# Where the first four activation tiles begin in on-chip memory: 96 instead of 128 modulo 256 bytes

## The chip, the core and the metric

The kernel runs on one core of one Trainium2 chip. The metric is the device time of one execution in microseconds, as the median over runs. TensorE does the matrix products, VectorE, ScalarE and GpSimd the elementwise work, and SyncE issues most of the DMAs. A granted clock of 1.00 in the profile is TensorE's upper level, 2.4 GHz; the lower one is 1.2 GHz.

## What is computed

Two transformer blocks run over one sequence of 256 positions of width 2048, everything in float32. The first mixes by pooling and a gated delta rule, attends to a memory of 256 rows, and ends in a gated feed-forward layer of width 5632. The second mixes by two sparse attentions and ends in a feed-forward layer of width 8192. Cut to its large products:

```python
x = x + hybrid_mixer(rms_norm(x, g1), w_in, ...) # h @ w_in, then y @ w_mix_out
x = x + memory_cross_attention(rms_norm(x, g2), mem_h, w_xq, w_xkv, w_xo)
x = x + (silu(causal_dwconv(h @ w_gate, cw, cb)) * (h @ w_up)) @ w_down
x = rms_norm(x, final_norm_g)
...
o = concat([nsa_mixer(...), moba_mixer(...)]) @ w_o    # inputs from h @ w_in_2
x = x + gate_m * rms_norm_2(o, post_norm_mix)
x = x + gate_f * rms_norm_2(square(relu(h @ w_up_2)) @ w_down_2, post_norm_ffn)
```

## The kernel before

**Products.** Every large product is made of three single-pass products in the type float32r: each operand is split into a high part and a low remainder, and high x high, high x low and low x high are summed in PSUM. Weights arrive by DMA in units of 128x1024 float32 (`load_to`, L202), ScalarE writes the high part `wh` (L216), VectorE the low part `wl` (L218).

**Two ways round.** `lin_b` (L316 to L318) has a 128x128 block of the weights as the stationary operand and streams 256 columns of an activation row past it: `wh` against the high part of the activations, `wh` against the low part, `wl` against the high part. `lin_a` (L298 to L300) has 128 columns of the activations as the stationary operand and streams 512 columns of `wh` or `wl` past them (256 in the last two groups of three layers). Each matmul is preceded by its own weight load, which the profile lists as engine PEld. A group is one block of 512 output columns; over a contraction of 2048 it has 192 matmuls in `lin_b` and 96 in `lin_a`.

**Activation tiles.** `act_pair(0)` hands out the tiles A0 to A3 (high part in A0 and A1, low part in A2 and A3), `act_pair(1)` the tiles A4 to A7. Each is 128x8x256 of float32, 8192 bytes in a partition, and a row that `lin_b` streams is 1024 bytes of it. A0 to A3 hold the input of `w_in`, of `w_xq`, of `w_gate` and `w_up`, of `w_in_2` and of `w_up_2`, which all go through `lin_b` except the `z`, `nv` and `mv` parts; they also hold the mixer's output, which is the stationary operand of `w_mix_out`. A4 to A7 hold the lifted memory (streamed by the four groups of keys, `mk`, and stationary for `mv`), the attention outputs and the hidden units of both feed-forward layers, which are stationary in `w_xo`, `w_down`, `w_o_2` and `w_down_2`.

**Places.** The pool gives every name its bytes in the order in which the program first asks for it, rounded up to 32 bytes in a partition, and keeps them. Counted so, the built program puts `mhalf` at byte 54400, `c_first` at 54432, the three columns `c_G1`, `c_G2` and `c_GP` (64 bytes each, asked for early, L572, and used much later) at 54464, 54528 and 54592, then A0 at 54656, which is 128 modulo 256. A1, A2 and A3 follow without a gap, so that all their rows begin at 128 modulo 256. Then come `c_mix_p` and `c_mem_p` (32 bytes each), and A4 at 87488, which is 192 modulo 256; so are A5, A6 and A7. The three buffers of `wh` and the three of `wl` all begin at 192 modulo 256, and a stationary block in them is 512 bytes further each.

**Order.** Instructions are written in the order in which they run on each engine. While a group's matmuls are issued, `pump` slips in pieces of the other work (the evacuation of earlier groups, the adaptive gains, the delta rule).

Of the kernel before, what the change touches and what calls it, by code (L numbers as in the profile page):

```python
# [18 lines left out]
KB = D // P  # L19
# [71 lines left out]
class Prog:  # L91
# [407 lines left out]
    def run(self):  # L499
# [69 lines left out]
        self.mhalf = self.pool.tile([P, 8], F32, name="mhalf")  # L569
        nc.gpsimd.memset(self.mhalf, -0.5)  # L570
        nc.scalar.activation(self.col("first", 8), self.mhalf, AF.Copy)
        for name in ("G1", "G2", "GP"):  # L572
            self.col(name, KB)


        self.split_to(1)
# [9 lines left out]
        def stats():  # L586
            nc.sync.dma_start(cst, i["cst"])
            for c in range(4):
                nc.sync.dma_start(self.X[:, :, c * 512:(c + 1) * 512], xsrc[:, :, c * 512:(c + 1) * 512])
                yield  # L590
            self.load_small(w_in, 5120, 16, "ba", "s9")
            for n in ("dn_a_log", "dn_dt_bias"):
                t = self.named[n] = self.col(n, 8)
                sv = i[n]
                nc.sync.dma_start(t, bass.AP(tensor=sv.tensor, offset=sv.offset, ap=[[0, P], [1, 8]]))
            self.load_const("early")
            for c in range(4):
                for tb in range(2):
                    self.sq_sum(self.X[:, tb, c * 512:(c + 1) * 512], parts[:, tb, c:c + 1])
                yield  # L600
            yield from self.rms_task("mix_r", parts, "rr")
            msrc = i["mem"][0].rearrange("(b p) d -> p b d", p=P)
            for c in range(4):
                mt = self.t("r7", [P, 2, 512])
                nc.gpsimd.dma_start(mt, msrc[:, :, c * 512:(c + 1) * 512])
                for _ in range(3):
                    yield
                for tb in range(2):
                    self.sq_sum(mt[:, tb], mparts[:, tb, c:c + 1])
            self.rcm = self.rms_cols("mem_r", mparts)  # L610
            yield
            self.rrm = yield from self.row_bcast(self.rcm, "rrm", 1)

        st = self.start(stats())
        A4 = self.t("A4", [P, 2, 4, T])
        A5 = self.t("A5", [P, 2, 4, T])
        for name in ("silu_c", "gl16"):
            self.col(name, KB)
        S = [{"k": A4[:, 0], "q": A4[:, 1], "v": A5[:, 0]}, {}]
        self.z = [None, None]  # L620
# [650 lines left out]
    def ffn1(self, xh, xl, ready, rt):  # L1271
# [6 lines left out]
        def ups(s):  # L1278
            hid[s] = self.hidden(["A4", "A6"] if s % 2 else ["A5", "A7"])
            j = 0  # L1280
            for c in self.slabs[s]:
                self.lin_b(self.gate[c], xh, xl, lambda a, c=c: self.chain(self.wait_for(rt), self.gate_evac(a, c)),
                           ready=ready if c == 0 else None)
                self.lin_b(self.up[c], xh, xl, lambda a, c=c, j=j: self.up_evac(a, c, j, hid[s]))
                j += 4
# [141 lines left out]
    def mixer2(self):  # L1427
# [48 lines left out]
        ev = self.lin_a(b2["nv"], xh, xl, lambda a: self.copy2_evac(a, vsw))  # L1476
        o0h, o0l = self.hidden(["A4", "A6"])
        att = []
# [401 lines left out]
    def ffn2(self):  # L1880
# [8 lines left out]
        def ups(s):  # L1889
            hid[s] = self.hidden(["A4", "A6"] if s % 2 else ["A5", "A7"])  # L1890
            for c in range(2 * s, 2 * s + 2):
                self.lin_b(self.up2[c], xh, xl, lambda a, c=c: self.relu_evac(a, c, hid[s]),
                           ready=ready if c == 0 else None)
# [89 lines left out]
```

## Time and profile before

| what | us |
|---|---|
| median of 3 runs | 2738.76 |
| lowest and highest run | 2735.97, 2741.46 |
| the profiled execution | 2730.08 |
| its span, first to last instruction | 2728.3 |
| PE busy within the span | 2678.7 |

The profiled execution is one more run. Its time is its span plus 1.8 us; it lies 8.7 us below the median. In the profile PE counts a matmul from its start to its end, and neighbouring matmuls overlap; how fast a stream of them runs is read from the distance between their starts, called the pitch below.

### The profile page before, as it was taken

How to read it: one execution, taken by the hardware profiler on the slowest of the kernel's cores; microseconds unless marked ns; L12 is line 12 of the kernel's file. 1: busy time of each engine (PE TensorE's matmuls, PEld its weight loads, DVE VectorE, ACT ScalarE, POOL GpSimd, SP SyncE). 2: the span in 40 equal slices, each digit the busy share in tenths (PEclk: the TensorE clock that was granted, in tenths of full speed). 3: DMA queues.
4: the chain of work that ended last, by engine and by line, in shares of the span. 5: the costliest groups of instructions: out<-in, count | busy, mean ns of one | idle time of the engine just before them, and what ended most of it. 6: DMA issues, size and time to landing. Idle time of an engine off the chain costs nothing.

```text
span 2728.3 us, 45974 instructions
## 1 busy us (share of the span) xinstructions
PE 2678.7 (98%) x18466; PEld 2476.8 (91%) x18466; DVE 1852.9 (68%) x2327; ACT 1303.5 (48%) x1924; POOL 256.4 (9%) x234
## 2 busy tenths in 40 slices
PE   8999999999999999999999989999989999999998
PEld 8999998889989999999999789997889988999897
DVE  6665745677688877777877576677675566655555
ACT  6544533454455454444444554444554444444443
POOL 0230211000000021000000001001011000000020
PEclk9999999999999999999999999999989999999999
DMA  8644644688788888888887656544557767766654
GB/s 293 197 131 132 187 123 141 217 295 274 225 269 273 284 262 262 280 271 267 287 265 256 196 157 179 147 147 131 170 178 234 237 218 239 233 191 192 189 186 151
DMA packets 293127, 584.33 MB, mean 214 GB/s; under 512 B 21921, under 2 KB 36385, under 8 KB 292913
## 3 DMA queue, kind: packets, MB, share of 16 engines
q1 hardware_dynamic: 288528, 568.41, 65.4%
q0 software_dynamic: 3664, 11.67, 1.4%
q8 instruction: 145, 2.38, 0.3%
q10 hardware_dynamic: 720, 1.31, 0.1%
q14 instruction: 70, 0.57, 0.1%
HBM read 579.21 MB, written 2.10 MB: 213 GB/s over the span
## 4 chain that ended last, share of the span: by engine, by line
PE 91%; DVE 3%; ACT 2%; issue 2%; DMA 1%; POOL 1%; SPq 0%; DVEq 0%; POOLq 0%; ACTq 0%
PE acc L316 16%; PE acc L318 16%; PE acc L317 16%; PE acc L298 12%; PE acc L299 12%; PE acc L300 12%; DVE wl L218 1%; ACT wh L216 1%; DMA w<-w_in 1%; PE m L996 1%; PE m L1049 1%; PE m L1056 1%; ACT dd L376 1%; PE m L1146 1%; PE m L1115 1%
## 5 line engine op out<-in xcount | busy, mean ns | idle before, releaser
L218 DVE TENSOR_TENSOR wl<-w,wh 128x1024 fp32r<-128x1024 f32 x880 | 1096.2, 1248 | 811.6 <-ACT wh L216 809.6
L216 ACT ACTIVATE wh<-w 128x1024 fp32r<-128x1024 f32 x880 | 928.1, 1058 | 1111.3 <-PE acc L317 603.3
L316 PE MATMUL acc<-A,wh 128*128 128x256 f32 x3968 | 1122.6, 283 | 9.4 <-ACT A L404 7.7
L318 PE MATMUL acc<-A,wl 128*128 128x256 f32 x3968 | 1111.3, 280 | 6.2 <-DVE wl L218 6.2
L317 PE MATMUL acc<-A,wh 128*128 128x256 f32 x3968 | 1111.0, 280 | 0.7 <-DVE A L1423 0.7
L318 PEld LDWEIGHTS acc<-A,wl 128*128 128x128 f32 x3968 | 756.2, 191 | 8.0 <-DVE wl L218 8.0
L316 PEld LDWEIGHTS acc<-A,wh 128*128 128x128 f32 x3968 | 749.7, 189 | 11.4 <-ACT A L404 7.7
L317 PEld LDWEIGHTS acc<-A,wh 128*128 128x128 f32 x3968 | 749.3, 189 | 2.6 <-DVE A L1423 1.2
L298 PE MATMUL acc<-wh,A 128*128 128x512 f32 (+1 forms) x1584 | 616.0, 389 | 0.3 <-DVE r L1262 0.3
L299 PE MATMUL acc<-wl,A 128*128 128x512 f32 (+1 forms) x1584 | 608.0, 384 | 1.1 <-DVE wl L218 0.9
L300 PE MATMUL acc<-wh,A 128*128 128x512 f32 (+1 forms) x1584 | 607.7, 384 | 0.0
L299 PEld LDWEIGHTS acc<-wl,A 128*128 128x128 f32 x1584 | 298.1, 188 | 60.2 <-DVE wl L218 4.2
L300 PEld LDWEIGHTS acc<-wh,A 128*128 128x128 f32 x1584 | 297.7, 188 | 59.3
L298 PEld LDWEIGHTS acc<-wh,A 128*128 128x128 f32 x1584 | 297.9, 188 | 57.2 <-issue 0.9
L1198 DVE SCALAR_TENSOR_TENSOR r<-r,c_silu_c,r 128x1024 f32<-128x1024 f32 x128 | 170.0, 1328 | 0.0
L1874 POOL TENSOR_TENSOR s<-s 128x512 f32<-128x512 f32 x32 | 51.0, 1592 | 582.5 <-ACT s L1873 582.5
L1198 DVE SCALAR_TENSOR_TENSOR s<-s,c_silu_c,s 128x512 f32<-128x512 f32 x128 | 95.8, 748 | 13.7 <-DMA s<-w_ada 12.4
L1253 POOL TENSOR_TENSOR r<-r,rr 128x1024 f32<-128x1024 f32 x11 | 27.8, 2532 | 565.7 <-ACT r L1252 565.7
L1718 ACT ACTIVATE s<-s,c_am 128x128 f32<-128x128 f32 (+1 forms) x48 | 21.5, 448 | 92.0 <-DVE c_am L1716 92.0
L1606 POOL TENSOR_TENSOR r<-r,s 128x512 f32<-128x512 f32 x15 | 25.6, 1704 | 269.6 <-DVE s L1603 269.6
L1249 DVE SCALAR_TENSOR_TENSOR r<-r,prm,r 128x254 f32<-128x254 f32 x88 | 42.4, 481 | 1.6
L376 ACT ACTIVATE dd<-X 128x512 bf16<-128x512 f32 (+1 forms) x42 | 25.5, 608 | 36.1 <-DVE X L1458 16.1
(376 smaller groups left out, 1611.0 us busy)
## 6 DMA issues: line engine op xcount, KB each, us to landing
w<-w_up SPq DMA_DIRECT2D x216, 512.0 KB, 3.8
w<-w_down SPq DMA_DIRECT2D x216, 512.0 KB, 4.0
w<-w_in SPq DMA_DIRECT2D x152, 512.0 KB, 3.7
r<-w_ada SPq DMA_DIRECT2D x128, 512.0 KB, 5.1
w<-w_gate SPq DMA_DIRECT2D x88, 512.0 KB, 4.2
w<-w_xkv SPq DMA_DIRECT2D x64, 512.0 KB, 3.9
s<-w_ada SPq DMA_DIRECT2D x128, 256.0 KB, 5.2
w<-w_mix_out SPq DMA_DIRECT2D x32, 512.0 KB, 3.7
```

The lines of the kernel that those rows point to most:

```text
L216: nc.scalar.activation(hi[:, :m], src[:, :m], AF.Copy)
L218: eng.tensor_tensor(lo[:, :m], src[:, :m], hi[:, :m].bitcast(F32), op=OP.subtract)
L298: mm(ps, h, wh[:, k, :], start=kb == 0, stop=False)
L299: mm(ps, h, wl[:, k, :], start=False, stop=False)
L300: mm(ps, lo, wh[:, k, :], start=False, stop=kb == g.nkb - 1)
L316: mm(ps, wb, h, start=kb == 0 and b % 2 == 0, stop=False, skip_group_check=True)
L317: mm(ps, wb, lo, start=False, stop=False, skip_group_check=True)
L318: mm(ps, wb2, h, start=False, stop=kb == g.nkb - 1, skip_group_check=True)
L376: self.nc.scalar.activation(junk[:, :src.shape[-1]], src, AF.Square, accum_out=out)
L1198: nc.vector.scalar_tensor_tensor(acc, tiles.pop(n), self.silu_c[:, kb:kb + 1], acc, op0=OP.mult, op1=OP.add)
L1249: nc.vector.scalar_tensor_tensor(cv[:, b, s:], st[:, b, :T - s], w[k], cv[:, b, s:], op0=OP.mult, op1=OP.add)
L1874: nc.gpsimd.tensor_tensor(y, y, y, op=OP.mult)
```

## The change

Two of the early requests are exchanged. Of the three columns ahead of A0 the third, `GP` (64 bytes), is replaced by `ffn_p` (32 bytes), a column that is otherwise asked for much later; `GP` is now placed where the program first uses it. So A0 to A3 begin 32 bytes earlier, at 54624 and on, which is 96 modulo 256. After A3 and the two columns that follow it, `xa_p` (32 bytes) is asked for ahead of A4, so that A4 stays at 87488. The remaining small columns shift by 32 or 64 bytes; `mod` is among them, at 96 modulo 256 instead of 128. All other large tiles, `wh`, `wl` and the landing buffers of the weights keep their places. On every engine the instructions, their order and their waits are the same as before.

```diff
@@ -569,8 +569,8 @@
         self.mhalf = self.pool.tile([P, 8], F32, name="mhalf")
         nc.gpsimd.memset(self.mhalf, -0.5)
         nc.scalar.activation(self.col("first", 8), self.mhalf, AF.Copy)
-        for name in ("G1", "G2", "GP"):
-            self.col(name, KB)
+        for name, n in (("G1", 16), ("G2", 16), ("ffn_p", 8)):
+            self.col(name, n)
@@ -612,6 +612,8 @@
         st = self.start(stats())
+        for name, n in (("xa_p", 8),):
+            self.col(name, n)
         A4 = self.t("A4", [P, 2, 4, T])
         A5 = self.t("A5", [P, 2, 4, T])
```

## Rows read from the trace of the kernel before

**Rows 1.** The page, parts 1 and 2: busy time, granted clock.

```profile
PE 2678.7 (98%) x18466; PEld 2476.8 (91%) x18466; DVE 1852.9 (68%) x2327; ACT 1303.5 (48%) x1924; POOL 256.4 (9%) x234
...
PEclk9999999999999999999999999999989999999999
```

**Rows 2.** The page, part 4: the chain that ended last, by engine, line.

```profile
PE 91%; DVE 3%; ACT 2%; issue 2%; DMA 1%; POOL 1%; SPq 0%; DVEq 0%; POOLq 0%; ACTq 0%
PE acc L316 16%; PE acc L318 16%; PE acc L317 16%; PE acc L298 12%; PE acc L299 12%; PE acc L300 12%; DVE wl L218 1%; ACT wh L216 1%; DMA w<-w_in 1%; PE m L996 1%; PE m L1049 1%; PE m L1056 1%; ACT dd L376 1%; PE m L1146 1%; PE m L1115 1%
```

**Rows 3.** The page, part 5: count, busy us, mean ns, idle before.

```profile
L316 PE MATMUL acc<-A,wh 128*128 128x256 f32 x3968 | 1122.6, 283 | 9.4 <-ACT A L404 7.7
L318 PE MATMUL acc<-A,wl 128*128 128x256 f32 x3968 | 1111.3, 280 | 6.2 <-DVE wl L218 6.2
L317 PE MATMUL acc<-A,wh 128*128 128x256 f32 x3968 | 1111.0, 280 | 0.7 <-DVE A L1423 0.7
...
L298 PE MATMUL acc<-wh,A 128*128 128x512 f32 (+1 forms) x1584 | 616.0, 389 | 0.3 <-DVE r L1262 0.3
```

**Rows 4.** Tile A: count, durations in ns, first and last start; three stretches.

```profile
L316 PE MATMUL acc<-A,wh x64: 276/276/367, 31.8 to 55.0; 128*128 128x256 f32 x64
...
L317 PE MATMUL acc<-A,wh x220: 276/276/276, 1394.8 to 1469.3; 128*128 128x256 f32 x110
...
L318 PE MATMUL acc<-A,wl x64: 276/276/276, 2427.8 to 2449.3; 128*128 128x256 f32 x64
```

**Rows 5.** The same view, four other stretches.

```profile
L317 PE MATMUL acc<-A,wh x31: 281/281/281, 84.3 to 94.9; 128*128 128x256 f32 x31
...
L316 PE MATMUL acc<-A,wh x254: 281/281/281, 980.3 to 1069.7; 128*128 128x256 f32 x127
...
L318 PE MATMUL acc<-A,wl x126: 281/281/281, 2137.8 to 2181.9; 128*128 128x256 f32 x126
...
L317 PE MATMUL acc<-A,wh x63: 281/281/281, 2604.7 to 2626.6; 128*128 128x256 f32 x63
```

**Rows 6.** Timeline of PE in the keys' first group: start us, duration us.

```profile
299.83 0.28 PE L317 MATMUL acc<-A,wh 128*128 128x256 f32 x1
...
300.19 0.28 PE L317 MATMUL acc<-A,wh 128*128 128x256 f32 x1
...
300.55 0.28 PE L317 MATMUL acc<-A,wh 128*128 128x256 f32 x1
...
300.91 0.28 PE L317 MATMUL acc<-A,wh 128*128 128x256 f32 x1
```

**Rows 7.** Tile A in the last group, 256 weight columns wide.

```profile
L298 PE MATMUL acc<-wh,A x16: 283/283/283, 2710.7 to 2716.1; 128*128 128x256 f32 x16
```

**Rows 8.** Chain in order of time, a `w_down_2` group: start us, us, what.

```profile
2094.16 0.23 PE acc L298
...
2104.36 0.23 PE acc L298
```

**Rows 9.** The same view, a `w_mix_out` group.

```profile
497.08 0.23 PE acc L298
...
507.38 0.23 PE acc L298
```

**Rows 10.** Lines L258 and L260, a small projection, 65 to 76 us.

```profile
L258 PE MATMUL m<-A,s x12: 276/276/276, 65.8 to 73.7; 128*32 128x256 f32 x12
...
L260 PE MATMUL m<-A,s x12: 276/276/276, 65.9 to 73.8; 128*16 128x256 f32 x12
```

**Rows 11.** Busy time by engine in two stretches of `w_gate` and `w_up`.

```profile
core 0: us, PE busy (x) PEld busy (x) DVE busy (x) ACT busy (x) POOL busy (x), PEclk, DMA share, GB/s
870.00:956.00 86.00, 86.00 (x761) 86.00 (x761) 71.39 (x75) 42.15 (x46) 4.30 (x3) 1.00 0.86 294
980.00:1070.00 90.00, 90.00 (x765) 89.92 (x764) 72.01 (x72) 41.99 (x46) 8.95 (x5) 1.00 0.84 271
```

**Rows 12.** Waits of PE: us in total, times, longest.

```profile
PE acc L316 <- ACT A L404: 7.7, 1, 7.7
...
PE acc L318 <- DVE wl L218: 6.2, 9, 0.8
```

## The prediction

> **What bounds the kernel now.** Read the busy shares and the chain first. PE is busy for 2678.7 of 2728.3 us at the upper clock level [rows 1], the chain is 91% PE, and 48% of it is the three lines of `lin_b`, 36% those of `lin_a` [rows 2]. PE hardly waits: the two largest waits of these lines are 7.7 us, once at the start, and 6.2 us in nine pieces [rows 12]. In the gate and up stages VectorE is busy 71.4 of 86 us and ScalarE 42.2 [rows 11]. `lin_b` has 3968 matmuls in each of its three lines [rows 3], 11,904; 768 of them are the keys', and 11,136 stream A0 to A3. So the time is the number of matmuls times their pitch, and the change can act only on that pitch: there is nothing else in it.
>
> Next, the pitch itself. The 256-column matmuls of `lin_b` with A0 to A3 have two pitches. In some stretches each lasts 276 ns and 220 of one line start within 74.5 us: 74.5 / 219 / 3 = **113.4 ns** [rows 4]. In others it is 281 ns, and (1069.7 - 980.3) / 253 / 3 = **117.8 ns** [rows 5]. Tiles, code and clock are the same; a stretch keeps its pitch over whole groups, and a change mostly falls where the stream was interrupted. Taking the view group by group, 22 of the 58 groups that stream A0 to A3 are at the short pitch (the first and last are in rows 4) and 36 at the long one (first and last in rows 5): 22 x 192 = 4224 and 36 x 192 = 6912 matmuls.
>
> **Why a start address can matter here.** Four places differ in where the two operands begin. I write the distance as stationary start minus streaming start, in bytes.
> - Distance 0, both at 192: the keys stream A4 to A7 against `wh`; three matmuls take 0.36 us, 120.0 ns each [rows 6]. The last group streams 256 columns of `wh` against A4 to A7: (2716.1 - 2710.7) / 15 / 3 = 120.0 ns [rows 7]. With 512 columns it is (2104.36 - 2094.16) / 15 / 3 = 226.7 ns [rows 8]. The 256 further columns cost 106.7 ns, 0.417 ns each, so that a fixed 13.3 ns, or 32 columns, come on top of each matmul.
> - Distance +64 (stationary `wh` at 192, A0 to A3 streaming at 128): 113.3 or 117.8 ns, so the fixed part is 6.7 or 11.1 ns, and 64 bytes (16 columns, 6.7 ns) have saved all of themselves or a third.
> - Distance -64 (stationary A0 to A3 at 128, `wh` streaming at 192): (507.38 - 497.08) / 15 / 3 = 228.9 ns [rows 9], a fixed part of 15.6 ns: a third of 64 bytes on top.
>
> An estimate from these rows: the fixed part falls with the distance, by its full column time in the short mode and a third of it in the long one. A place of its own speaks against it: the small projection loads 32 or 16 stationary columns from 192 and 64 in turn, and streams A0 to A3 at the short 276 ns throughout [rows 10] (its tile `s10` begins at 192, and each step is 128 bytes). That the stationary start counts at all rests on rows 9 against rows 8.
>
> The Trainium skill says otherwise ("TensorE: Matmul & The Clock Gate", Part 2, step-by-step): TensorE reads the streaming operand and the next weights through two independent ports, and loading does not take bandwidth from the running matmul. By that the start of the streaming operand alone would count, which is the first rival below; rows 8 and 9, which share the streaming start and differ by 2.3 ns, do not agree with it.
>
> **The change part by part.**
> 1. *A0 to A3 streaming at 96 in `lin_b`.* The distance becomes +96, 24 columns or 10.0 ns. Short mode: 13.3 - 10.0 = 3.3 ns, pitch 110.0, which is 3.33 ns less for 4224 matmuls: -14.1 us. Long mode: 13.3 - 10.0 / 3 = 10.0 ns, pitch 116.7, 1.11 ns less for 6912: -7.7 us. No row has a start that is not a multiple of 64, so the bounds lie at the nearest rows and past them. Above: the 120.0 ns of distance 0 [rows 6]. Below: 106.7 ns, no fixed part at all, 11,136 matmuls x (116.1 now on the mean - 106.7) = -105 us. I take the value that continues the rows, because 96 is the near neighbour of 128.
> 2. *A0 to A3 stationary at 96 in `lin_a`.* `z0`, `z1`, `w_mix_out`, `nv` and two `mv` groups have 192 + 384 + 288 = 864 matmuls. The distance goes from -64 to -96, another sixth of 6.7 ns: +1.1 ns, +1.0 us. Bounds: -2.3 ns (distance 0) and +6.7 ns, -2 to +6 us.
> 3. *ScalarE and VectorE writing the rows of A0 to A3, and the moved columns.* These are the same instructions; VectorE has some 15 us in 86 to spare [rows 11]. The columns are single small operands. I cost them at nothing; without that cover, VectorE's 71.4 us would have to grow by a fifth before it set the pace.
>
> Sum: -14.1 - 7.7 + 1.0 = **-20.8 us**. On the profiled execution 2730.1 - 20.8 = 2709.3; the median was 8.7 us above that execution, which is what some 2000 matmuls more at the long pitch would cost (2000 x 4.45 = 8.9). Since the share of modes is that of one execution, I put the gain on the median: 2738.8 - 20.8 = **2718**. Its own range, with a share of the short mode (now 4224 of 11,136) from a fifth to a half and 6.67 ns between the modes, is 2709 to 2731.
>
> **The rivals.**
> - *A start off the 64-byte grid costs a whole extra piece* (slower). Against streaming at 128, streaming at 192 adds 6.7 ns to the short pitch, and both are multiples of 64; 96 is halfway into such a piece. If what counts is the streaming start alone and any start that is not a multiple of 128 reads one piece more, A0 to A3 behave like A4 to A7 in rows 6: 120.0 ns. 4224 x 6.67 + 6912 x 2.22 = 28.2 + 15.3 = +43.5 us, 2782. If the unused 96 bytes count in full (24 columns over the 6.7 ns at 128, 16.7 ns, pitch 123.3): 4224 x 10 + 6912 x 5.56 = +80.6, 2819. For it: the exact 120.0 with two streaming operands. Against: rows 9. It decides from a pitch above 116.1, today's mean.
> - *The modes change, the pitches do not.* All groups short: 6912 x 4.45 = -30.8 us, 2708; all short at 110.0 ns: -67.9, 2671. All long at 117.8: 4224 x 4.45 = +18.8, 2757. For it: the same code has both modes, so a small push decides which is entered. Against: nothing says which way.
> - *Nothing happens at 32 bytes*: 2739. The Trainium skill gives on-chip memory lines of 16 bytes ("SBUF — State Buffer", Specifications); 96 and 128 both begin such a line, and by it alone the change would do nothing. The rows with 128 and 192, both such starts too, differ by 6.7 ns. What speaks for this rival in the rows is that the small projection kept one pitch over two stationary starts [rows 10].
>
> **How the numbers follow.** Forecast (both modes a little shorter) 0.32, 2709 to 2731; the short mode takes all 0.18, 2671 to 2708; all long 0.08, 2757; the extra piece at 120.0 ns 0.20, 2782, and at 123.3 ns 0.08, 2819; nothing 0.14, 2739. About 0.2%, 5.5 us, is what a measurement of this kernel can tell from no change. Faster: 0.32 x 0.95 + 0.18 = 0.48; same: 0.14 + the edge of the forecast = 0.16; slower: 0.08 + 0.28 = 0.36. The range 2675 to 2790 leaves out the all-short end (0.05), 123.3 ns (0.08) and some 0.05 of what is not listed.
>
> **What would show it.** In the same view of tile A, calm stretches of `lin_b` with durations below 276 ns and a pitch near 110.0, others near 116.7, and the `w_mix_out` group near 230 ns, show steps 1 and 2 right. A single duration of 283 ns and a pitch of 120.0 in the gate and up stages show the extra piece. 276 and 281 unchanged, with other shares, show that only modes moved. The pitch of `w_down` and `w_down_2` (226.7) and of the keys (120.0) must not change in any case, since A4 to A7 and `wh` stay. The prediction is wrong if the streaming start alone counts, or if VectorE's or ScalarE's writes to A0 to A3 slow enough to make PE wait.

## The result, and the profile after

The change makes the kernel slower: the median goes from 2737.38 (four runs, the three of above and one more) to **2755.18 us**, a ratio of **1.0064**, with a 95% interval of 1.0047 to 1.0082. I had forecast 2718. The four runs after lie between 2754.99 and 2757.21; the runs of before in the same comparison between 2735.97 and 2741.46. The profiled execution after took 2755.07 us, its span is 2753.2. Against the span of before, 2728.3, that is +24.9 us; the medians differ by 17.8, because the profiled execution of before lay 7.3 us below its median and that of after lies at its own.

The page of the kernel after, part 1 and the clock of part 2, as in [rows 1]:

```profile
PE 2705.9 (98%) x18466; PEld 2500.1 (91%) x18466; DVE 1852.7 (67%) x2327; ACT 1303.7 (47%) x1924; POOL 255.4 (9%) x234
...
PEclk9999999999999999999999999999999999999999
```

PE is busy 27.2 us longer in as many instructions, at the same clock; VectorE, ScalarE and GpSimd are busy as long as before, to 1 us. PE does not wait longer: its waits (us in total, times, longest), the two that [rows 12] shows, are

```profile
PE acc L316 <- ACT A L404: 7.7, 1, 7.7
...
PE acc L318 <- DVE wl L218: 5.5, 9, 0.8
```

Part 5 of the page (count, busy us and mean ns, idle before), as in [rows 3]:

```profile
L316 PE MATMUL acc<-A,wh 128*128 128x256 f32 x3968 | 1127.5, 284 | 9.2 <-ACT A L404 7.7
L318 PE MATMUL acc<-A,wl 128*128 128x256 f32 x3968 | 1116.4, 281 | 5.5 <-DVE wl L218 5.5
L317 PE MATMUL acc<-A,wh 128*128 128x256 f32 x3968 | 1115.9, 281 | 0.7 <-DVE A L1425 0.7
...
L298 PE MATMUL acc<-wh,A 128*128 128x512 f32 (+1 forms) x1584 | 617.1, 390 | 0.3 <-DVE r L1264 0.3
```

So the time went where the prediction said that it had to go, into the pitch of `lin_b`, but with the other sign. Tile A in four calm stretches of the kernel after, that is, with nothing slipped in between the matmuls (count, durations shortest/median/longest, first and last start): a `w_up` group, a `w_up_2` group, a `w_mix_out` group, a `w_down` group:

```profile
L317 PE MATMUL acc<-A,wh x65: 277/281/283, 1015.8 to 1038.6; 128*128 128x256 f32 x65
...
L317 PE MATMUL acc<-A,wh x65: 277/280/282, 2070.4 to 2092.9; 128*128 128x256 f32 x65
...
L299 PE MATMUL acc<-wl,A x16: 392/392/392, 502.2 to 512.7; 128*128 128x512 f32 x16
...
L298 PE MATMUL acc<-wh,A x16: 389/389/389, 1107.2 to 1117.4; 128*128 128x512 f32 x16
```

The single durations of 276 and 281 ns [rows 4, 5] are gone; one stretch now mixes 277 to 283. The pitch is (1038.6 - 1015.8) / 64 / 3 = **118.7 ns** in the first and (2092.9 - 2070.4) / 64 / 3 = **117.2 ns** in the second; in before both groups were at the long pitch, 117.8. All 32 calm groups that stream A0 to A3 sit near one of these two values (26 at 118.7 and 6 at 117.3 by their means), and they are not the long and the short ones of before: of ten groups that were short, seven are now at 118.7 and three at 117.3. `w_mix_out` went from 228.9 [rows 9] to 10.5 / 15 / 3 = 233.3 ns. `w_down` keeps 10.2 / 15 / 3 = 226.7 ns [rows 8], and the keys keep 120.0: in the timeline (start, duration)

```profile
303.39 0.28 PE L317 MATMUL acc<-A,wh 128*128 128x256 f32 x1
...
303.75 0.28 PE L317 MATMUL acc<-A,wh 128*128 128x256 f32 x1
...
304.11 0.28 PE L317 MATMUL acc<-A,wh 128*128 128x256 f32 x1
```

Summed over groups, each from its first to its last start, after minus before:

| groups | us |
|---|---|
| the 22 groups of `lin_b` that were short before (4224 matmuls) | +16.9 |
| the 36 that were long (6912) | +5.8 |
| `lin_a` with A0 to A3 stationary (864) | +1.0 |
| `lin_a` with A4 to A7, and the keys | +1.1 |
| the rest, between the groups | +0.1 |
| span | +24.9 |

### The profile page after: what moved, and what is told of

Read it like the earlier page. It is cut to its first block, busy times and chain, and to the rows that moved or that the text cites. A ratio compares the mean times of both kernels' runs of the same rounds, so it can differ in the third digit from the quotient of the medians.

```text
span 2753.2 us, 45974 instructions
## 1 busy us (share of the span) xinstructions
PE 2705.9 (98%) x18466; PEld 2500.1 (91%) x18466; DVE 1852.7 (67%) x2327; ACT 1303.7 (47%) x1924; POOL 255.4 (9%) x234
## 4 chain that ended last, share of the span: by engine, by line
PE 89%; DVE 4%; ACT 2%; issue 2%; DMA 1%; POOL 1%; SPq 1%; DVEq 0%; POOLq 0%; ACTq 0%
PE acc L316 16%; PE acc L318 16%; PE acc L317 16%; PE acc L298 12%; PE acc L299 12%; PE acc L300 11%; DVE wl L218 2%; ACT wh L216 1%; PE m L998 1%; PE m L1051 1%; DMA s<-w_ada 1%; PE m L1058 1%; DMA w<-w_in 1%; ACT dd L376 1%; PE m L1117 1%
## 5 line engine op out<-in xcount | busy, mean ns | idle before, releaser
L317 PE MATMUL acc<-A,wh 128*128 128x256 f32 x3968 | 1115.9, 281 | 0.7 <-DVE A L1425 0.7
L317 PEld LDWEIGHTS acc<-A,wh 128*128 128x128 f32 x3968 | 750.8, 189 | 2.6 <-DVE A L1425 1.2
```

What stands on the lines that cost most here:

```text
L317: mm(ps, wb, lo, start=False, stop=False, skip_group_check=True)
```

## The experiments

The kernels differ from before in the list of columns that are asked for ahead of A0 and ahead of A4, and in the size of a tile called `spare`, allocated ahead of the weight buffers: with 48 floats of it `wh` and `wl` begin at 192 modulo 256, each 8 floats less move them down by 32 bytes. "Distance" is the prediction's: stationary start minus streaming start, counted modulo 256. The theory that I carried from the result was that this distance decides; the rival, that the streaming start alone does. Each kernel up to the distance of +80 ran once. Beside it stands before on the same chip: one run of 2735.98 us for the first three kernels and for the start at 64, one of 2734.63 for the other four, and for +80 the median of 13 runs, 2735.82. Runs of before alone lie between 2730 and 2742 us, so that a single time says something from about 10 us on; the pitches are read from the traces.

**The moved columns alone.** Four columns ahead of A0, so that it stays at 128:

```diff
-        for name in ("G1", "G2", "GP"):
-            self.col(name, KB)
+        for name, n in (("G1", 16), ("G2", 16), ("ffn_p", 8), ("xa_p", 8)):
+            self.col(name, n)
```

> The small columns move as in the change (GP late, ffn_p and xa_p ahead of A0, mod at 96), but A0 to A3 stay at 128 modulo 256. If the tiles' start is the cause, lin_b has the two pitches of before, 113.3 and 117.8 ns, the w_mix_out groups 229 ns, and the time is that of before (2736 to 2741 us). If a moved column is the cause, the pitches of the change, 117.3 and 118.7 ns, or its time, 2755 us, come back.

Measured: 2733.8 us against 2735.98, and both pitches of before. The same view, a `w_up` group and a stretch at the short duration:

```profile
L317 PE MATMUL acc<-A,wh x64: 280/281/282, 1006.6 to 1028.8; 128*128 128x256 f32 x64
...
L317 PE MATMUL acc<-A,wh x220: 275/276/281, 1394.8 to 1469.7; 128*128 128x256 f32 x110
```

(1028.8 - 1006.6) / 63 / 3 = 117.5 ns, the long pitch; the second stretch has an interruption in it, and its calm groups are at 113.3. The moved columns cost nothing that shows; the start of A0 to A3 is the cause.

**The change, and the weights 32 bytes lower too.** A0 to A3 at 96 as in the change, `wh` and `wl` at 160: distance +64 again.

```diff
-        for name in ("G1", "G2", "GP"):
+        for name, n in (("G1", 16), ("G2", 16), ("ffn_p", 8)):
...
+        for name, n in (("xa_p", 8),):
...
-        self.pool.tile([P, 48], F32, name="spare")
+        self.pool.tile([P, 40], F32, name="spare")
```

> The change, with wh and wl (and the landing buffers) 32 bytes earlier too, at 160: A0 to A3 still begin at 96, but the distance from streaming to stationary start is +64 again. If the distance decides: lin_b back at 113.3 and 117.8 ns, w_mix_out back at 229 ns; the keys (distance -32) above 120 ns, near 121 to 123; w_down and w_down_2 (distance +32) below 226.7 ns, near 223 to 226; about 2715 to 2735 us. If the start of the streaming operand alone decides: lin_b stays at 117.3 and 118.7 ns, keys at 120.0, and all lin_a groups move alike to one new pitch.

**The other way.** A0 to A3 stay at 128, `wh` and `wl` go to 224: distance +96 without the change.

```diff
-        self.pool.tile([P, 48], F32, name="spare")
+        self.pool.tile([P, 56], F32, name="spare")
```

> The kernel before, with wh and wl 32 bytes later, at 224: A0 to A3 stay at 128, the distance becomes +96 as in the change. If the distance decides: lin_b at 117.3 and 118.7 ns and w_mix_out at 233.4 ns as after the change; the keys (distance +32) below 120 ns, w_down and w_down_2 (distance -32) above 226.7, near 228; 2755 to 2765 us. If the streaming start alone decides: lin_b at 113.3 and 117.8 ns.

Measured: 2736.9 us for the first, 2777.35 for the second. First kernel, a `w_up`, a `w_up_2` and a `w_down` group; then the second kernel, a `w_up` and a `w_down` group:

```profile
L317 PE MATMUL acc<-A,wh x65: 276/276/276, 1006.0 to 1027.8; 128*128 128x256 f32 x65
...
L317 PE MATMUL acc<-A,wh x65: 281/281/281, 2165.5 to 2188.1; 128*128 128x256 f32 x65
...
L299 PE MATMUL acc<-wl,A x16: 395/396/396, 1095.0 to 1105.5; 128*128 128x512 f32 x16
```

```profile
L317 PE MATMUL acc<-A,wh x65: 276/281/283, 1018.7 to 1041.5; 128*128 128x256 f32 x65
...
L299 PE MATMUL acc<-wl,A x16: 393/394/397, 1110.8 to 1121.3; 128*128 128x512 f32 x16
```

With A0 to A3 at 96 and the distance back at +64, the two pitches of before return: 21.8 / 64 / 3 = 113.5 and 22.6 / 64 / 3 = 117.7 ns. With A0 to A3 untouched and the distance at +96, the pitch is 22.8 / 64 / 3 = 118.7, that of the change. This settles it: the distance decides, not the place of either operand alone. (The landing buffers of the weights move with `wh` and `wl`, but PE's waits are those of before.) Both kernels pay in `w_down`, where A4 to A7 stayed and the weights moved: 10.5 / 15 / 3 = 233.3 ns in place of 226.7, some 19 us over all groups of `lin_a` with A4 to A7. That is why the first, whose `lin_b` with A0 to A3 is 11.5 us quicker than in the profile of before, does not gain. Here the expectations missed: 223 to 226 ns at distance +32 and 228 at -32 were too low, the keys at -32 ran near 116.7 and not above 120, and the second kernel came out 12 us above its range.

**All large operands 32 bytes lower**, so that every distance stays (the change without `xa_p` ahead of A4, and `spare` with 40 floats, so that A4 to A7, `wh` and `wl` are at 160).

> The change with A4 to A7 and wh and wl 32 bytes earlier as well: every large operand begins off the 64-byte grid (96 and 160), and all distances are those of before. If the distance alone decides: 113.3 and 117.8 ns, keys 120.0, w_mix_out 229, w_down 226.7, 2725 to 2741 us by the share of the two pitches. If a start off the 64-byte grid costs by itself: 117.3 and 118.7 ns or more in lin_b and 233.3 ns in lin_a, 2755 to 2775 us.

Measured: 2731.75 us against 2734.63, a `w_up` group at each pitch:

```profile
L317 PE MATMUL acc<-A,wh x65: 281/281/281, 1007.1 to 1029.7; 128*128 128x256 f32 x65
...
L317 PE MATMUL acc<-A,wh x65: 276/276/276, 1431.3 to 1453.0; 128*128 128x256 f32 x65
```

117.7 and 113.0 ns (113.3 by the mean over the group) with every start at 32 modulo 64, and the calm groups of `w_down` stay at 226.7: the change's place for A0 to A3 costs nothing as long as the rest moves along.

**Other starts of A0 to A3**: 64, 192 and 160, so distances of +128, 0 and +32, by other lists of columns ahead of A0 (in the first of them `GP` comes ahead of A4 instead; A4 to A7 and the weights stay at 192):

```diff
-        for name in ("G1", "G2", "GP"):
+        for name, n in (("G1", 16), ("G2", 16)):
```

```diff
+        for name, n in (("G1", 16), ("G2", 16), ("GP", 16), ("mix_p", 8), ("mem_p", 8)):
```

```diff
+        for name, n in (("G1", 16), ("G2", 16), ("GP", 16), ("mem_p", 8)):
```

> A0 to A3 at 64 modulo 256, distance +128, everything else as before. If the fixed part has its lowest value near +64 and rises on either side: lin_b at 118 to 120 ns, 2755 to 2780 us. If it is a matter of the 64-byte grid alone: pitches of multiples of 64 again, 113.3 and 117.8 or 120.0 ns. If it falls with the distance as I forecast: below 113 ns.

> A0 to A3 at 192, distance 0 to wh and wl, everything else as before. If the distance decides: every calm lin_b stretch at 120.0 ns, like the keys before, without a second pitch; w_mix_out at 226.7 ns like w_down; about 2777 to 2783 us. If the streaming start decides in another way than rows 6 show: another pitch.

> A0 to A3 at 160, distance +32. If any distance off the 64-byte grid behaves alike: lin_b near 117 to 119 ns with some jitter, and w_mix_out (distance -32) at 233.3 ns, as after the change; 2750 to 2765 us. If the pitch falls evenly from distance 0 to +64: 116.7 ns, 2740 to 2745 us, and w_mix_out near 228 ns.

Measured: 2767.03, 2768.54 and 2754.51 us. One `w_up` group of each, in this order:

```profile
L317 PE MATMUL acc<-A,wh x65: 283/284/285, 1018.4 to 1041.4; 128*128 128x256 f32 x65
```

```profile
L317 PE MATMUL acc<-A,wh x65: 283/283/283, 1016.9 to 1039.9; 128*128 128x256 f32 x65
```

```profile
L317 PE MATMUL acc<-A,wh x64: 277/280/285, 1015.6 to 1038.0; 128*128 128x256 f32 x64
```

23.0 / 64 / 3 = 119.8 ns at +128 and at 0 (120.0 by the mean of all its pitches), and 22.4 / 63 / 3 = 118.5 at +32. The second time is 8 us below its expectation, though the pitches are the expected ones, `w_mix_out` at 226.7 included. So the pitch is no line in the distance: it falls from 120.0 at 0 over 118.3 at +32 to 113.3 or 117.8 at +64, and is back at 117.3 or 118.7 at +96 and near 120 at +128. The two points that the prediction had, 0 and +64, were the top and the bottom of a dip.

**A4 to A7 at 0 modulo 256**, the last two distances: the weights stay, `GP` stays ahead of A0, and `silu_c` and 16 floats of padding move A4 to A7 up by 64 bytes.

```diff
+        for name, n in (("silu_c", 16),):
+            self.col(name, n)
         A4 = self.t("A4", [P, 2, 4, T])
...
+            self.pool.tile([P, 16], F32, name="pad6")
...
-        self.pool.tile([P, 48], F32, name="spare")
+        self.pool.tile([P, 32], F32, name="spare")
```

> A4 to A7 at 0 modulo 256, A0 to A3 and wh and wl as before: the distance in w_down, w_down_2, w_xo, w_o_2 and mv goes from 0 to +64, the one that lin_b has; that of the keys to -64. If lin_a gains from it as lin_b does: 220.0 or 224.4 ns instead of 226.7 in 3600 matmuls, 8 to 24 us less, 2712 to 2730 us; keys near 122 ns. If equal starts are the best that lin_a can have: 229 ns as in w_mix_out, some 8 us more, 2744 us.

Measured: 2740.1 us against 2734.63, which is neither of the two expectations. A `w_down` group (stationary A, distance +64, 512 columns) and the last group (the same with 256 columns):

```profile
L299 PE MATMUL acc<-wl,A x16: 394/394/394, 1092.6 to 1103.1; 128*128 128x512 f32 x16
...
L298 PE MATMUL acc<-wh,A x16: 276/276/276, 2721.1 to 2726.2; 128*128 128x256 f32 x16
```

The same two tiles, the same distance: 5.1 / 15 / 3 = 113.3 ns with 256 columns, where before had 120.0 [rows 7], and 10.5 / 15 / 3 = 233.3 ns with 512, where before had 226.7 [rows 8]. The distance that is best for a stream of 256 columns is among the worst for one of 512. In the trace `lin_a` with A4 to A7 takes 18.7 us more than in before, and `lin_b` with A0 to A3 8.6 less, because more of its groups began at the short pitch.

**Between +64 and +96.** A0 to A3 as one tile, sliced 12 floats in, so that its rows begin at 112: distance +80. `GP` is asked for late and `spare` has 32 floats, so that A4 to A7 and the weights stay.

```diff
+        if half == 0:
+            big = self.t("A0", [P, 32 * T + 16], F32R)
+            a = [big[:, 12 + j * 8 * T:12 + (j + 1) * 8 * T].rearrange("p (k t) -> p k t", k=8) for j in range(4)]
...
```

> A0 to A3 as one tile whose rows begin at 112 modulo 256, wh and wl at 192, so a distance of +80 in lin_b and -80 in lin_a, between the +64 of before (113.3 and 117.8 ns) and the +96 of the change (117.3 to 118.7). One tile in place of four may add waits of some us where a stage ends. Theory A (the short pitch belongs to multiples of 64 alone, anything between costs more): 117 to 119 ns like +96, 2750 to 2758. Theory B (the pitch rises steadily with the way from +64, 4 ns over 32 bytes in the short mode): about 115.3 short and 118.2 long, 2742 to 2748.

Measured: 2764.28 us, above both expectations; 32.9 of the 34.2 us that its span lies above that of before are `lin_b` with A0 to A3, so that it is no wait of the larger tile:

```profile
L317 PE MATMUL acc<-A,wh x65: 281/285/288, 1017.7 to 1040.6; 128*128 128x256 f32 x65
```

22.9 / 64 / 3 = 119.3 ns, more than at +96. The dip at +64 is narrow on this side: 16 bytes further the pitch is almost that of distance 0. So a line through +64 and +96 would have been wrong as well.

**The two pitches at +64, and a kernel that beats both.** In the traces so far a `lin_b` group that PE enters straight from `lin_a` at 226.7 ns starts at the long pitch (in before 11 of 12; the twelfth came from the slower `nv` group), and four transposes slipped into a long group (L1177) made it short, at six places of before with a calm stretch on either side. (With other placements not always: in four other traces at distance +64 two long stretches stayed long and three short ones became long.) In the kernel with A0 to A3 at 96 and the weights at 160, where that `lin_a` ran at 233.3, 11 of 12 began short. The long `w_up_2` row shown there is the group behind the twelfth, and the `w_up` row the group behind one of the eleven; both kept the pitch of the entry. If the entry decides, a foreign matmul at the entry can change it. I put one, two or four transposes of the identity into the accumulator that the group then restarts, ahead of the first matmul of a `lin_b` group that follows a `lin_a` group (17 places; here for one; the first line stands in `lin_a`, the others in `lin_b`):

```diff
+        self.after_a = True
...
+            if self.after_a:
+                self.after_a = False
+                for r in range(1):
+                    self.nc.tensor.transpose(accs[0][:, r * P:(r + 1) * P], self.c("ident"), self.c("ident"))
```

> The kernel of before with one 128x128 transpose (the identity matrix against itself, into the accumulator that the group then restarts) ahead of the first matmul of each lin_b group that follows a lin_a group, some 15 places, about 0.12 us each, so +2 us of work. Theory: at distance +64 the pitch of a calm stretch is set by how the stream was entered; a lin_b group entered from lin_a at 226.7 ns starts at the long pitch of 117.8 ns and keeps it until the stream is interrupted. If one foreign matmul is interruption enough, the groups after lin_a start at 113.3 ns: up to 27 long groups of 192 matmuls x 4.45 ns = -23 us, +2 us, about 2715 to 2725. Rival (the mode comes from something else, such as what VectorE or the transfers do in that stretch): the same long groups, 2735 to 2742.

> As brk1, with four such transposes in place of one, which is what ended the long pitch within a group in the kernel before at seven places (the four transposes of L1177). Work added: 15 x 4 x 0.11 = +6.5 us. Theory: the groups after lin_a start short, -23 + 6.5, about 2718 to 2728. If one transpose is not enough but four are, brk1 is at 2738 to 2742 and this one below 2730. Rival: the modes are not set by the entry, 2742 to 2748.

> As brk1 with two transposes in place of one. One of them made 9 of the 12 groups entered directly from lin_a start short, four made none of 12, none left 11 of 12 long. If what counts is the time by which the entry is shifted (each transpose adds about 0.11 us), two may land on either pitch: all short would give 27 x 192 x 4.45 = -23 us and +3.5 us for the transposes, about 2716 to 2722; none short 2738 to 2743. If the count of foreign matmuls mattered only as an interruption, two could not be worse than one: at most 2725.

Measured, as ratios to before with 95% intervals: one transpose **2722.87 us, 0.9946 (0.9931 to 0.9961)**; two 2735.35, 0.9999 (0.9988 to 1.001); four 2738.79, 1.001 (1.0 to 1.0021). One came out as expected; four missed the 2718 to 2728 of its theory. Between the two profiled executions one transpose gains only 4.6 us of span, since that of before lies 5.7 us below the 2735.82 of this comparison and that of one transpose 2.6 above its median. Tile A in the same four groups of `w_gate` and `w_up` with one and then with four (the lines of the code are shifted; L324 is L317):

```profile
L324 PE MATMUL acc<-A,wh x256: 276/276/283, 986.4 to 1073.1; 128*128 128x256 f32 x128
```

```profile
L324 PE MATMUL acc<-A,wh x256: 281/281/281, 987.2 to 1077.3; 128*128 128x256 f32 x128
```

86.7 / 255 / 3 = 113.3 against 90.1 / 255 / 3 = 117.8 ns, where before had 117.8 [rows 5]. Of the 12 entries straight from `lin_a`, 9 are short with one transpose, 3 with two, none with four, 1 in before. The timeline of one such entry (start, duration), in before, with one transpose and with four:

```profile
980.12 0.39 PE L300 MATMUL acc<-wh,A 128*128 128x512 f32 x1
980.34 0.28 PE L316 MATMUL acc<-A,wh 128*128 128x256 f32 x1
```

```profile
985.93 0.40 PE L303 MATMUL acc<-wh,A 128*128 128x512 f32 x1
986.17 0.27 PE L316 MATMUL acc<-cst 128*128 128x128 f32 x1
986.20 0.37 PE L323 MATMUL acc<-A,wh 128*128 128x256 f32 x1
986.40 0.28 PE L324 MATMUL acc<-A,wh 128*128 128x256 f32 x1
```

```profile
986.44 0.40 PE L303 MATMUL acc<-wh,A 128*128 128x512 f32 x1
...
987.04 0.36 PE L323 MATMUL acc<-A,wh 128*128 128x256 f32 x1
```

That the entry sets the pitch is shown. That an interruption as such makes it short is not: by that, two and four transposes could not be worse than one. One transpose shifts the entry by about 0.04 us, four by 0.37, and the traces say how fine the moment counts. Take the time from the last start of `lin_a` to the first of `lin_b`, to the nanosecond, in the five traces at distance +64 without added transposes, 60 entries: 37 of at most 229 ns began long, of two of 230 one began long and one short, 20 of 231 to 236 began short, and one of 240 long. With two transposes 368 to 371 ns began short, and 365 and 372 to 375 long; with four all lay at 588 to 593, long; with one, 261, 265 and 266 began short, and 257, 263 and 264 long. This is a pattern in the traces, not an experiment, and why some moments give the short pitch stays open.

## Why the prediction was wrong

- **The bound was right.** Only the pitch could move the time, and 22.7 of the 24.9 us are `lin_b` with A0 to A3, at the upper clock level, with no new wait.
- **The variable was right.** That the distance between the two operands decides was an inference from rows 6 to 9; the pair at +64 and +96 with exchanged places, and the kernel with everything moved, show it. Why the distance matters inside the chip, no run here shows. With it falls the first rival's reason, that the streaming start alone counts: the streaming operand of `w_down` did not change its place between the kernel with A4 to A7 at 0 and before, and the pitch is 233.3 against 226.7. The Trainium skill ("TensorE: Matmul & The Clock Gate", Part 2, step-by-step) has it that loading the next weights takes no read bandwidth from the running matmul; what I drew from that, that the place of the weights would not count, does not hold in this case.
- **The step that failed is part 1's choice, "I take the value that continues the rows, because 96 is the near neighbour of 128".** It drew a line through two distances, 0 and +64, and read off +96: -14.1 us for the short mode and -7.7 for the long one. Measured: +16.9 and +5.8, per matmul +4.0 ns in place of -3.3, and +0.8 in place of -1.1; the pitch at +96 is 117.3 or 118.7 ns, not 110.0 and 116.7. The pitch is lowest in a narrow dip at +64 and has risen again at +80. The rows had starts at multiples of 64 alone, as the text said; what lay between and beyond was not theirs to tell. The small projection, which spoke against the line [rows 10], should have had more weight: its stationary blocks lie at +64 and at -64 in turn, and no line gives both one duration.
- **Part 2** was +1.0 us and came out at +1.0, by luck: the calm `w_mix_out` groups went up by 4.4 ns, not 1.1, and `w_mix_out`, `z` and `nv` together by 2.6 us, but the two groups of `mv`, which have much other work between their matmuls, came out 1.6 us shorter.
- **Part 3** was right: the moved columns cost nothing, and PE waits no longer for the writes to A0 to A3 than before.
- **The rivals.** The piece that would cost 120.0 ns does exist, at distance 0 and not at the change: with A0 to A3 at 192 the sum of `lin_b` was 40.2 us above that of before, near the rival's 43.5. But 64, 96 and 160 are no multiples of 128 either, and they did not all cost 120.0: at 96 the pitch was 113.3 or 117.8 once the weights had moved along. "All long at 117.8", 2757, gave nearly the measured time by another way: no calm group has that pitch, and the modes did not all become long but drew together, at 117.3 and 118.7. "Nothing" fell: a shift of two of the 16-byte lines that the Trainium skill names ("SBUF — State Buffer", Specifications) changed the pitch of every calm group that streams A0 to A3, by 0.4 to 5.4 ns, although 96, 128 and 112 all begin such a line.
- **The scatter** fits its reading, that the share of the short mode differs from run to run: the runs of before spread over some 10 us, and with the two pitches 1.4 ns apart in place of 4.5, the four runs after spread over 2.2. It is not shown, since before has one trace; and the four runs with one transpose, which still have both pitches, spread over 3.5.

## What to carry to other kernels

In this kernel a stream of float32r matmuls that alternate with weight loads has a pitch that depends on the start of the stationary operand relative to that of the streaming one. In another kernel, measure that table for the sizes that it has, and do not extend it by a line. Moving one group of tiles changes the distance in every product that they take part in, so the gain in one (256 columns) has to be set against the loss in another (512 columns). Where the same code shows two steady pitches, look at how the stream was entered: one small matmul at the entry was worth 13 us here, more than any placement that I tried. Two and four were worth nothing, so this too has to be measured each time.

## What the runs showed of the hardware that I had not expected

The pitch in ns of back-to-back float32r matmuls with a 128x128 weight load each, at the upper clock level, in calm groups of these kernels (means over a group; 256 columns at -64 over calm stretches of the keys), by the distance in bytes:

| distance | 256 columns | 512 columns |
|---|---|---|
| 0 | 120.0 | 226.7 |
| +32, -32 | 118.3, 116.7 | 233.4, 233.3 |
| +64 | 113.3 or 117.8 | 233.3 |
| -64 | 117.8 | 228.9 |
| +80, -80 | 119.3, - | -, 230.0 |
| +96, -96 | 117.3 or 118.7, - | -, 233.3 |
| +128, -128 | 120.0, some 118.7, - | -, 232.2 |

At +64 two steady pitches, 4.5 ns apart, hold over whole groups; which one is entered changes with the entry. At +32, +80 and +96 the durations within a group vary (276 to 288 ns), where at 0 they are all alike and at +64 alike within 1 ns or so, at either pitch.
